# A state space stage re-ordered: its recurrence for two groups in complex pairs, its inputs turned inside SBUF, and modulations in four columns

## The chip, the cores and the metric

The kernel runs on one core of one Trainium2 chip. The metric is the device time of one execution in microseconds (us). The engines are TensorE (PE, matrix products), VectorE (DVE), ScalarE (ACT), GpSimd (POOL) and SyncE (SP, which only issues transfers here).

## The reference, cut to what matters

Two blocks work on 256 tokens of 1024 features, beside a context of 256 tokens. The change lies in the first block. Its first layer is an attention with 16 heads (MLA), its second is a state space layer (S5) with 128 groups of 64 complex states; one direction runs forward, one backward, and each runs through the context first and then through the tokens:

```python
for i in range(2):
    sh, sc, gt = split(silu(c) @ w_mod[i] + b_mod[i], 3)      # modulation, 1024 -> 3072
    h = x * (1 + sc) + sh                                     # also for the context, with c_ctx
    y = mla(h) if i == 0 else s5(h)
    x = layernorm(ALPHA * x + gt * y)

def s5(h):
    u, g = split(h @ w_in, 2)            # 1024 -> 2048 inputs u, 2048 gates g
    for direction in (forward, backward):
        x_t = lam_bar * x_{t-1} + b_bar @ u_t       # 128 groups x 64 complex states
        y  += real(c @ x_t)
    return ((ya * sigmoid(yb)) * silu(g)) @ w_out   # ya, yb = split(gelu(y) @ w_glu + b_glu, 2)
```

## The kernel before

**Products.** Activations and weights are split into a high and a low half in a reduced float32 format, and each product is three matmuls (`products`, lines 119 to 121: high by high, low by high, high by low). `weight` (line 88) fetches 512 KB of a weight with SyncE, ACT casts the high half (`wh`, line 97), DVE subtracts it (`wl`, line 98). The third matmul of each three needs `wl`.

**Modulation.** `mod` (line 577) multiplies silu(c) (32 columns, two of them used) by the weights `w_mod` in pieces of 256 KB. A piece is one matmul of 512 columns (part 0) or two of 256 (part 1), written to 32 rows of PSUM each. There are 64 pieces: 16 of part 1 for the first layer, worked off in the stage `mla_in`, and 48 for the second layer (32 of part 0, 16 of part 1) worked off between the heads. The start of the kernel does the first layer's part 0 with four matmuls of 128 columns in four column groups (`shift_scale`, line 678).

**The S5 stage.** Time is cut into blocks of 8 tokens: 32 blocks of context and 32 of tokens. The 128 groups are worked off in four parts b = 0..3 with four quarters a = 0..3 each:

- `u(b, j)` (line 1072): 48 matmuls make a 512 x 512 corner of the inputs, ACT copies it to SBUF (`s5_ut`, line 438) and stores it to DRAM (`d_u`, line 439); a transfer of GpSimd's queue loads it back in another layout (`s5_U`, line 446).
- `s5_blocks` (line 454): with operators loaded from DRAM (`s5_op<-d_rt`) 128 matmuls per quarter pair make the block sums, and ACT copies each bank to `s5_V` (line 475). The operators share one ring of five buffers with those of the outputs.
- `s5_scan` (line 480): the recurrence over the 63 blocks, on DVE. Real and imaginary parts lie apart, 32 columns of 63 blocks. A tree of 5 levels runs over the context, then seven single steps, then four steps of eight blocks with a table of powers (`s5_tab`, made by `s5_steps`, line 316). It takes 80 instructions a part (lines 493 to 497), and two copies (line 517).
- `s5_out` (line 520): `within` (line 536) adds what a block's own tokens give, `across` (line 549, operators `d_o`) what the states give, `close` turns the result back.

The emission order of PE and DVE is kept as written. `s5_layer` (line 1078) interleaves each scan with the next part's `u`, with `s5_blocks`, with the output of the part before, and with single gates (`gate`, line 955: 24 matmuls, stored to DRAM as `d_sg`). A scan runs right after its blocks, so that `across(b-1)` stands beside scan b. ACT and the queues follow a scheduler. After the last scan stand `across` of part 3 and the first product of the GLU.

## Time and profile before

| what | us |
|---|---|
| median of 3 runs | 1473.43 (1468.22 to 1474.59) |
| the profiled execution | 1472.76 |
| its span on the core | 1471.0 |
| start | 0 to 60 |
| `mla_in` | 60 to 216 |
| heads, with the second layer's modulation | 216 to 520 |
| layer norm, S5 inputs of part 0 | 520 to 612 |
| S5 stage | 612 to 858 |
| GLU | 858 to 1050 |
| second block | 1050 to 1471 |

The stages are read from the times at which their lines first run. Over the span PE is busy 92%, DVE 78%, ACT 48%, POOL 7%, and PE's mean granted clock is 0.958 of full speed. A busy share over a stage says how far an engine is from being its limit; which wait ended last there is read from the chain of waits and from the timeline.

### The profile page before, as it was taken

Reading aid. Unit: us, or ns where it says so; the run is one execution under the profiler, and the core shown is the slowest. Engines: PE = TensorE matmul, PEld = TensorE weight load, DVE = VectorE, ACT = ScalarE, POOL = GpSimd, SP = SyncE. Lnnn points to the kernel's source line nnn. Section 1 sums busy time; section 2 is a strip of 40 time slices with the busy share of each in tenths; the row PEclk is TensorE's granted clock in tenths of the full one; section 3 lists DMA queues with packets and bytes.
Section 4 is the critical chain, followed back from the end, with each engine's and each line's share of the span. In section 5 each row is a group of like instructions: output and inputs, shape, how many; then the busy total and the mean of one; then the engine's idle time right before and its main releaser. Section 6 shows DMA issues by size and latency. Waiting matters only on the chain.

```text
span 1471.0 us, 30448 instructions
## 1 busy us (share of the span) xinstructions
PE 1355.9 (92%) x12192; PEld 1199.6 (82%) x12192; DVE 1151.6 (78%) x2123; ACT 712.1 (48%) x1308; POOL 102.5 (7%) x225
## 2 busy tenths in 40 slices
PE   5979979999999998898787789999999999999997
PEld 4657657777788787898676689999999999999996
DVE  7989887888778889589988955655568876788887
ACT  4424336665455535432233354544347556655554
POOL 0012221111011101111111000000000000000000
PEclk8989998999999999999898889999999999999999
DMA  9469995555544543798778666566545453455552
GB/s 353 155 190 278 295 272 161 155 165 154 156 143 143 176 144 100 214 324 267 265 251 326 216 240 195 195 197 197 185 160 182 158 177 125 160 187 187 188 188 97
DMA packets 140623, 291.36 MB, mean 198 GB/s; under 512 B 30480, under 2 KB 70080, under 8 KB 135104
## 3 DMA queue, kind: packets, MB, share of 16 engines
q1 hardware_dynamic: 108592, 232.01, 47.5%
q0 software_dynamic: 11360, 49.34, 10.7%
q10 hardware_dynamic: 20528, 8.06, 2.0%
q8 instruction: 96, 1.57, 0.5%
q14 instruction: 47, 0.39, 0.1%
HBM read 234.83 MB, written 54.53 MB: 197 GB/s over the span
## 4 chain that ended last, share of the span: by engine, by line
PE 68%; DVE 14%; DMA 7%; issue 7%; ACT 3%; POOL 0%; SPq 0%; DVEq 0%; ACTq 0%; POOLq 0%
PE lin L121 14%; PE lin L120 14%; PE lin L119 14%; PE modps L591 3%; DVE s_t L493 2%; DVE wl L98 2%; DMA sp_x<-in_s_bcw_dram 2%; PE dn L121 1%; PE dn L119 1%; PE dn L120 1%; PE vps L472 1%; DMA d_o<-sp_o 1%; DVE s_V L495 1%; PE ptl L869 1%; PE slat L119 1%
## 5 line engine op out<-in xcount | busy, mean ns | idle before, releaser
L97 ACT CAST wh<-wr 128x1024 fp32r<-128x1024 f32 x268 | 280.7, 1049 | 412.1 <-PE lin L120 270.6
L98 DVE TENSOR_TENSOR wl<-wr,wh 128x1024 fp32r<-128x1024 f32 x268 | 327.7, 1224 | 150.4 <-ACT wh L97 149.8
L119 PE MATMUL lin<-prH,wh 128*128 128x256 f32 x512 | 145.9, 285 | 0.0
L119 PE MATMUL lin<-yaH,wh 128*128 128x256 f32 x512 | 145.5, 284 | 0.0
L121 PE MATMUL lin<-prH,wl 128*128 128x256 f32 x512 | 144.3, 282 | 1.0 <-DVE wl L98 1.0
L120 PE MATMUL lin<-yaL,wh 128*128 128x256 f32 x512 | 145.2, 284 | 0.0
L121 PE MATMUL lin<-yaH,wl 128*128 128x256 f32 x512 | 144.7, 283 | 0.0
L120 PE MATMUL lin<-prL,wh 128*128 128x256 f32 x512 | 144.3, 282 | 0.3 <-DVE prL L109 0.2
L120 PEld LDWEIGHTS lin<-prL,wh 128*128 128x128 f32 x512 | 97.3, 190 | 1.7 <-DVE prL L109 0.7
L119 PEld LDWEIGHTS lin<-prH,wh 128*128 128x128 f32 x512 | 97.4, 190 | 1.0
L119 PEld LDWEIGHTS lin<-yaH,wh 128*128 128x128 f32 x512 | 98.1, 192 | 0.0
L121 PEld LDWEIGHTS lin<-yaH,wl 128*128 128x128 f32 x512 | 98.1, 192 | 0.0
L120 PEld LDWEIGHTS lin<-yaL,wh 128*128 128x128 f32 x512 | 98.0, 191 | 0.0
L121 PEld LDWEIGHTS lin<-prH,wl 128*128 128x128 f32 x512 | 97.0, 189 | 1.2 <-DVE wl L98 1.2
L493 DVE TENSOR_TENSOR s_t<-s_V,s_tab 128x256 f32<-128x256 f32 (+2 forms) x120 | 73.0, 651 | 15.2 <-ACT s_V L475 13.9
L121 PE MATMUL u<-h,wl 128*128 128x256 f32 x224 | 65.1, 290 | 8.0 <-DVE wl L98 7.9
L121 PE MATMUL lin<-h,wl 128*128 128x256 f32 x128 | 43.3, 338 | 30.2 <-DVE wl L98 30.2
L427 POOL DMA_DIRECT2D d_t<-sp_g x128 | 66.8, 530 | 56.6 <-DVE sp_g L37 52.7
L120 PE MATMUL u<-h,wh 128*128 128x256 f32 x224 | 64.8, 289 | 1.6 <-issue 1.6
L119 PE MATMUL u<-h,wh 128*128 128x256 f32 x224 | 65.4, 292 | 0.0
L119 PE MATMUL lin<-hH,wh 128*128 128x512 f32 x144 | 61.7, 429 | 0.7 <-ACT hH L103 0.7
L37 DVE TENSOR_TENSOR sp_t<-s_pb,sp_x 128x1024 f32<-128x1024 f32 x64 | 60.2, 955 | 0.6
(505 smaller groups left out, 3862.2 us busy)
## 6 DMA issues: line engine op xcount, KB each, us to landing
wr<-in_glu_dram SPq DMA_DIRECT2D x64, 512.0 KB, 4.3
wr<-in_w_up_dram SPq DMA_DIRECT2D x44, 512.0 KB, 3.2
wr<-in_w_in_dram SPq DMA_DIRECT2D x32, 512.0 KB, 4.6
mraw<-in_w_mod_dram SPq DMA_DIRECT2D x64, 256.0 KB, 3.1
d_rt<-sp_rt SPq DMA_DIRECT2D x64, 256.0 KB, 4.1
d_o<-sp_o SPq DMA_DIRECT2D x32, 512.0 KB, 4.3
wr<-in_s_in_dram SPq DMA_DIRECT2D x32, 512.0 KB, 4.6
s_op<-d_o POOLq DMA_DIRECT2D x16, 1024.0 KB, 7.5
```

The lines of the kernel that those rows point to most:

```text
L37: return lambda *a, **k: self.net.in_order(f(*a, **k))
L97: self.in_order(nc.scalar.copy(hi, raw))
L98: self.in_order(nc.vector.tensor_tensor(lo, raw, hi.bitcast(F32), SUB))
L119: self.in_order(t.matmul(out, a[0], b[0], start=start, stop=False))
L120: self.in_order(t.matmul(out, a[0], b[1], start=False, stop=False))
L121: self.in_order(t.matmul(out, a[1], b[0], start=False, stop=stop))
L427: nc.gpsimd.dma_start(self.d_t[k].rearrange("s i j e c -> i s j e c")[:, :, j, e], a)
L472: self.in_order(nc.tensor.matmul(p[64 * e:64 * e + 64, c:c + 64], rt[:, d, j, r, 64 * e:64 * e + 64], u, start=True, stop=True, skip_group ...
L493: go(v.tensor_tensor(t[:, x], src.to_broadcast([128, 2, 32, n]), a[x].unsqueeze(1).to_broadcast([128, 2, 32, n]), MUL))
L495: go(v.tensor_tensor(dst, dst, t[:, 0], ADD))
L591: self.in_order(nc.tensor.matmul(p[32 * j:32 * j + 32, :w], self.cs[:, kc, :], raw[:, jj * w:jj * w + w], start=(kc == 0), stop=(kc == 7), ...
L869: self.in_order(nc.tensor.transpose(t[:, c], P[:, c], self.ident))
```

## The change

**Modulation.** The host lays `w_mod` out so that each piece of 256 KB is four blocks of 128 columns. `mod` issues four matmuls of 128 columns per piece, one to each group of 32 rows. The pieces, their bytes and their number are the same.

**The recurrence.** Real and imaginary part lie side by side (pairs of 8 bytes). A step is four DVE instructions: product with the real factor, sum, product of the swapped pair with the imaginary factor (with its signs), sum. `s5_context` runs the tree over the context of one part (five levels, 20 instructions on 1024, 512, 256, 128 and 64 elements); `s5_latents` runs 31 single steps for two parts together, 124 instructions on 128 elements each. All parts make 4 x 20 + 2 x 124 = 328 instructions; before there were 4 x 82.

**Inputs.** For parts 1 to 3 the store to `d_u` and the load of `s5_U` are replaced by eight SBUF to SBUF transfers per `u` on ACT's queue, 16 partitions each. Part 0 still goes through DRAM. `s5_ut` has one buffer there, where it had two.

**Order.** ACT copies each bank in two pieces (context sums to `s5_C`, the others to `s5_V`). The operators' ring has four buffers. All `u` and `s5_blocks` come first; `across` of parts 0 and 1 comes after the latents of the first pair, `across` of parts 2 and 3 after those of the second. Two clocks, estimates of PE's and of DVE's time, decide between which of them the DVE steps are emitted. Weights are fetched one or two products ahead, every second one of the first twelve into extra slots (`wx`). The 11 gates stand in the second half. The powers take 20 DVE and 16 ACT instructions, where there were 24 and 2.

```diff
-        hi, lo = (pool.tile([128, 1024], F32R, tag=tag + x, name=tag + x, bufs=bufs) for x in "hl")
+        if place is None:
...
+        hi, lo = place
         nc.sync.dma_start(raw, src)
...
+        for n, r, i in ((4, tr[:, :, 0], ti[:, :, 0]), (2, None, self.li)):
...
+                if r is not None:
+                    nc.scalar.copy(r[:, g].rearrange("p (d q) -> p d q", d=2), re)
+                for x in range(2):
+                    nc.scalar.mul(i[:, g, :, x].rearrange("p (d q) -> p d q", d=2), im, 2.0 * x - 1.0)
...
+        for k in range(4):
+            re, im = tr[:, :, k], ti[:, :, k, :, 1]
+            v.tensor_tensor(t[0], re, re, MUL)
+            v.tensor_tensor(t[1], im, im, MUL)
+            v.tensor_tensor(tr[:, :, k + 1], t[0], t[1], SUB)
+            for x in range(2):
+                v.scalar_tensor_tensor(ti[:, :, k + 1, :, x], re, 4.0 * x - 2.0, im, MUL, MUL)
...
-        nc.scalar.dma_start(self.d_u[b, j].rearrange("s p k -> p s k")[:, ::-1], ut.rearrange("p s g k -> p s (g k)"))
...
+    def s5_move_u(self, j, ps, U, tp):
+
+        ut = self.s5_turn_u(ps, tp, 1)
+        for s in range(8):
+            self.nc.scalar.dma_start(U[16 * s:16 * s + 16, j].rearrange("i q g k -> i (q g k)"),
+                                     ut[:, s].rearrange("p g k -> p (g k)"))
...
-        t = self.ops.tile([128, 2048], F32, name="s5_op", bufs=5)
+        t = self.ops.tile([128, 2048], F32, name="s5_op", bufs=4)
...
-                nc.scalar.copy(V[:, :, d, 4 * a:4 * a + 4, :].rearrange("p r q k -> p r (q k)"),
-                               p.rearrange("p (r c) -> p r c", r=2))
...
+            nc.scalar.copy(c[:, :, :, ::-1] if d else c, pv[:, :, :, 0:32])
+            nc.scalar.copy(x[:, :, :, 1 - d:32 - d], pv[:, :, :, 32 + d:63 + d])
+
+    def s5_step(self, a, src, swapped, t, base, dst):
+
+        v = self.nc.vector
+        for x, y, z in ((src, a[0], base), (swapped, a[1], dst)):
+            self.in_order(v.tensor_tensor(t, x, y.to_broadcast(t.shape), MUL))
+            self.in_order(v.tensor_tensor(dst, z, t, ADD))
...
+        for k in range(31):
+            c, o = (k, 31 - k), self.s5_column(V, (k + 1, 30 - k))
+            self.s5_step(a, self.s5_column(V, c), self.s5_column(V, c, swap=True), t, o, o)
+            yield 1.18
...
-                for q in range(4 * w // piece):
-                    raw = tp.tile([128, piece], F32, name="mraw", bufs=bufs)
-                    nc.sync.dma_start(raw, src[kc, :, q * piece:q * piece + piece])
...
+                for q in range(n):
+                    raw = tp.tile([128, 4, 128], F32, name="mraw", bufs=2)
+                    nc.sync.dma_start(raw, src[kc, q])
+                    for j in range(4):
                         self.in_order(nc.tensor.matmul(
-                            p[32 * j:32 * j + 32, :w], self.cs[:, kc, :], raw[:, jj * w:jj * w + w],
-                            start=(kc == 0), stop=(kc == 7), skip_group_check=True))
+                            p[32 * j:32 * j + 32, q * 128:q * 128 + 128], self.cs[:, kc, :], raw[:, j],
+                            start=(kc == 0 and q == 0), stop=(kc == 7 and q == n - 1), skip_group_check=True))
...
-            us = [self.u(1, j, h1) for j in range(2)]
             ahead = [self.operator(self.d_rt[a], nc.sync) for a in range(4)]
-            for j in range(2):
-                self.s5_store_u(1, j, us[j], tp)
-                self.s5_load_u(1, j, tp)
             self.s5_steps(tp)
             self.ordered = (mybir.EngineType.PE, mybir.EngineType.DVE)
-            st, prev = self.s5_blocks(0, tp, ahead), None
             for a in range(4):
-                st[2](a)
...
+                linear()
+                blocks(0, a)
+            linear()
+            within, across, close = out(0)
...
+            first = jobs[-1]
+            for a in range(4):
+                linear()
+                blocks(2, a)
+            linear()
+            for a in range(4):
+                blocks(3, a)
+                if a in (1, 2):
+                    linear()
+            last = jobs[-1]
+            scanned(first)
```

**DVE at the start of the S5 stage.** Before, from the last constants of the preparation (`sp_g`) on; the two `wl` are the low halves for `u(1, 0)` and `u(1, 1)`, and then comes the table of powers (`s_t` is its scratch tile, `s_tab` the table):

```order
L37 SCALAR_TENSOR_TENSOR sp_g<-dmask,dskip,sp_g 128x16 [waits Activation_49]
L98 TENSOR_TENSOR wl<-wr,wh 128x1024 [waits DMAHW6_49,PE_49,Activation_49]
L98 TENSOR_TENSOR wl<-wr,wh 128x1024 [waits DMAHW7_49,PE_49,Activation_49]
L332 TENSOR_TENSOR s_t<-s_tab 128x128 [waits DMASW7_49,DMAHW0_49,DMASW6_49,DMAHW2_49,DMASW5_49,DMAHW3_49,DMASW4_49,DMAHW4_49,DMASW3_49,DMAHW5_49,DMASW2_49,DMAHW6_49,DMASW1_49,DMAHW7_49,DMASW0_49,Activation_49]
L333 TENSOR_TENSOR s_t<-s_tab 128x128 [waits Activation_49]
L334 TENSOR_TENSOR s_tab<-s_t 128x128 [waits DVE_49]
```

After, the end of the powers (`s_tr` and `s_ti` are the new table) and the weights behind it; the first `wl` is that of `u(1, 0)`:

```order
L337 TENSOR_TENSOR s_t<-s_ti 128x128 [waits DVE_49]
L340 SCALAR_TENSOR_TENSOR s_ti<-s_tr,s_ti 128x4x32
L338 TENSOR_TENSOR s_tr<-s_t 128x4x32 [waits DVE_49]
L340 SCALAR_TENSOR_TENSOR s_ti<-s_tr,s_ti 128x4x32
L100 TENSOR_TENSOR wl<-wr,wh 128x1024 [waits PE_49]
L100 TENSOR_TENSOR wx<-wr,wx 128x1024
L100 TENSOR_TENSOR wl<-wr,wh 128x1024 [waits PE_49]
L100 TENSOR_TENSOR wx<-wr,wx 128x1024 [waits DMAHW1_49,Activation_49]
```

The `wl` of `u(1, 0)` stood ahead of the table; now it stands behind all 20 instructions of it, and the first of these still waits for the transfers of the stage ahead.

**ACT among the inputs.** Before, two inputs (`s_ut`, the copy in two pieces, and its store `d_u`) and the casts of weights between them:

```order
L438 COPY s_ut<-u 128x8x32 [waits DMAHW5_49,PE_49]
L438 COPY s_ut<-u 128x8x32
L439 DMA d_u<-s_ut 128x8x64 [waits DMAHW7_49,Activation_49]
L97 CAST wh<-wr 128x1024 [waits DMAHW5_49,DVE_49,PE_49]
L438 COPY s_ut<-u 128x8x32 [waits DMAHW2_49,PE_49]
L438 COPY s_ut<-u 128x8x32
L439 DMA d_u<-s_ut 128x8x64 [waits DMAHW1_49,Activation_49]
L97 CAST wh<-wr 128x1024 [waits DMAHW6_49,DVE_49,PE_49]
```

After, one input with its eight moves (`s_U<-s_ut`), and behind it a cast into an extra slot (`wx`) and the copies of block sums (`s_C`, `s_V`):

```order
L440 COPY s_ut<-u 128x8x32 [waits DMAHW4_49,DMAHW3_49,DMAHW5_49,DMAHW2_49,DMAHW6_49,DMAHW1_49,DMAHW7_49,DMAHW0_49,PE_49]
L440 COPY s_ut<-u 128x8x32
L99 CAST wh<-wr 128x1024
L458 DMA s_U<-s_ut 16x8x64 [waits Activation_49]
L458 DMA s_U<-s_ut 16x8x64 x5
L458 DMA s_U<-s_ut 16x8x64 [waits DMAHW2_49]
L458 DMA s_U<-s_ut 16x8x64 [waits DMAHW3_49]
L99 CAST wx<-wr 128x1024
L483 COPY s_C<-vps 128x2x128 [waits PE_49]
L484 COPY s_V<-vps 128x2x4x31
L483 COPY s_C<-vps 128x2x4x32 [waits PE_49]
```

The copy of an input now waits for the moves of the input ahead (`s_ut` has one buffer), the last of the eight moves waits for the first one's semaphore, and a cast and the copies of block sums stand behind them on ACT.

**PE between two parts.** Before, the blocks of part 2 (`vps`, from the inputs `s_U` and the operators `s_op`) stand behind a gate (`lin`):

```order
L119 MATMUL lin<-h_6368,wh 128x256
L120 MATMUL lin<-h_6368,wh 128x256
L121 MATMUL lin<-h_6368,wl 128x256
L472 MATMUL vps<-s_U,s_op 64x64 [waits DMASW5_49,DMASW4_49,PE_49]
L472 MATMUL vps<-s_U,s_op 64x64 x3
L472 MATMUL vps<-s_U,s_op 64x64 [waits DMASW6_49]
L472 MATMUL vps<-s_U,s_op 64x64
```

After, they stand right behind the last input of the part, `u(2, 3)`:

```order
L121 MATMUL u<-h_6827,wx 128x256
L122 MATMUL u<-h_6827,wx 128x256
L123 MATMUL u<-h_6827,wx 128x256
L477 MATMUL vps<-s_U,s_op 64x64 [waits DMAHW2_49,DMAHW3_49,DMAHW1_49,DMAHW5_49,DMAHW0_49,DMAHW6_49,DMASW1_49,DMAHW7_49,PE_49,Activation_49]
L477 MATMUL vps<-s_U,s_op 64x64
L477 MATMUL vps<-s_U,s_op 64x64 [waits DMAHW5_49,DMAHW4_49,DMAHW6_49,DMAHW3_49,DMAHW7_49,DMAHW1_49,DMAHW0_49]
L477 MATMUL vps<-s_U,s_op 64x64
```

The blocks' wait for their inputs moved from loads of an input made some products earlier to the moves of the product just ahead; part 3's blocks stand behind `u(3, 3)` in the same way, and part 1's last input has two outputs (`within`) behind it first.

## Rows read from the trace of the kernel before

**Rows 1.** Busy time by stage: the stretch in us from the span's start, its length, then for each engine the busy time and (x) its instructions, at the end PE's granted clock, the DMA engines' busy share and GB/s.

```profile
60.00:216.00 156.00, 136.62 (x1075) 98.94 (x1073) 135.44 (x204) 54.10 (x106) 33.00 (x76) 0.94 0.83 249
216.00:520.00 304.00, 301.06 (x2097) 229.88 (x2098) 249.45 (x461) 180.89 (x397) 30.67 (x69) 0.98 0.52 157
...
612.00:858.00 246.00, 196.16 (x3261) 182.15 (x3261) 199.97 (x383) 76.83 (x142) 28.40 (x51) 0.89 0.77 267
```

**Rows 2.** The chain of waits within 216 to 520 us (the heads), shares of these 304 us by engine and line.

```profile
by line: PE modps L591 12.7%; PE lin L119 6.2%; PE lin L120 6.0%; PE lin L121 6.0%; PE ptl L869 5.3%; PE slat L119 5.3%; PE slat L121 5.2%; PE slat L120 5.2%; PE rtps L400 4.4%; PE pv L119 4.2%; PE pv L120 3.5%; PE pv L121 3.5%; PE qabs L11
```

**Rows 3.** Timeline of PE (start in us, us, engine, line, operation, output<-inputs, shape, count; a float32 matmul is two records): four pieces of the start's modulation, then a piece of part 0 and a piece of part 1 in the heads, each with the matmul behind it.

```profile
33.91 1.08 PE L678 MATMUL modps<-mraw,cs 128*32 128x128 f32 x32
...
334.56 1.04 PE L591 MATMUL modps<-mraw,cs 128*32 128x512 f32 x2
335.53 1.09 PE L869 MATMUL ptl<-ident,P 128*128 128x128 f32 x8
...
492.40 0.63 PE L591 MATMUL modps<-mraw,cs 128*32 128x256 f32 x4
492.95 0.39 PE L119 MATMUL pv<-ptlH,ctH 128*128 128x256 f32 x1
```

**Rows 4.** The chain of waits within 60 to 216 us (`mla_in`), shares of these 156 us.

```profile
by line: DMA sp_x<-in_s_bcw_dram 14.5%; DMA d_o<-sp_o 11.5%; issue 9.5%; DVE sp_t L37 7.0%; DMA d_rt<-sp_rt 6.9%; DVE sp_o L37 6.2%; DVE sp_r L37 5.2%; PE lin L119 4.9%; PE lin L120 4.6%; PE lin L121 4.6%; DMA d_sg<-sg 4.2%; DVE wl L98 3.8%
```

**Rows 5.** Busy time in the four stretches from a scan's first instruction to its last (columns as in rows 1).

```profile
644.19:690.29 46.10, 41.27 (x513) 40.25 (x512) 45.24 (x88) 13.40 (x24) 8.40 (x15) 0.96 0.85 279
693.63:737.26 43.63, 32.94 (x517) 30.05 (x517) 42.70 (x86) 10.20 (x21) 5.16 (x10) 0.86 0.76 272
744.95:788.28 43.33, 31.64 (x592) 28.62 (x593) 42.40 (x86) 14.48 (x29) 5.16 (x10) 0.88 0.76 275
793.43:843.78 50.35, 36.08 (x513) 32.32 (x515) 48.03 (x91) 11.97 (x19) 3.76 (x7) 0.83 0.71 258
```

**Rows 6.** Groups of instructions by line and shape within the S5 stage (busy us, mean ns of one, idle time before them): `wl`, the gates' third matmuls, and the scan's products of 128 elements that lie a block column apart.

```profile
L121 PE MATMUL lin<-h,wl 128*128 128x256 f32 x88 | 31.1, 354 | 27.2 <-DVE wl L98 27.2
L98 DVE TENSOR_TENSOR wl<-wr,wh 128x1024 fp32r<-128x1024 f32 x25 | 30.5, 1218 | 14.8 <-ACT wh L97 14.8
...
L493 DVE TENSOR_TENSOR s_t<-s_V,s_tab 128x128 f32<-128x128 f32 x8 | 2.7, 381 | 0.1
```

**Rows 7.** Timeline of DVE: a chain of five dependent instructions on 128 elements; rows of the table of powers (single elements 32 bytes apart, then runs of two), each second of a pair reading what the first wrote; the `wl` and the scan behind it; what follows the last scan.

```profile
21.40 1.60 DVE L37 SCALAR_TENSOR_TENSOR lm_er<-lm_er,lm_sz 128x128 f32<-128x128 f32 x5
...
630.50 0.43 DVE L332 TENSOR_TENSOR s_t<-s_tab 128x128 f32<-128x128 f32 x1 [5.62 <-ACT s_tab L322]
...
631.29 0.41 DVE L334 TENSOR_TENSOR s_tab<-s_t 128x128 f32<-128x128 f32 x1
631.74 0.42 DVE L335 TENSOR_TENSOR s_t<-s_tab 128x128 f32<-128x128 f32 x1
...
633.32 0.42 DVE L333 TENSOR_TENSOR s_t<-s_tab 128x256 f32<-128x256 f32 x1
633.78 0.43 DVE L334 TENSOR_TENSOR s_tab<-s_t 128x256 f32<-128x256 f32 x1
...
641.87 1.21 DVE L98 TENSOR_TENSOR wl<-wr,wh 128x1024 fp32r<-128x1024 f32 x1
644.19 1.29 DVE L493 TENSOR_TENSOR s_t<-s_V,s_tab 128x512 f32<-128x512 f32 x2 [1.11 <-ACT s_V L475]
...
843.69 3.91 DVE L1132 TENSOR_TENSOR yaL<-y,yaH 128x512 fp32r<-128x512 f32 x6
```

**Rows 8.** Timeline of ACT and its queue (ACTq) at the start of the S5 stage.

```profile
616.82 1.05 ACT L97 CAST wh<-wr 128x1024 fp32r<-128x1024 f32 x1 [4.99 <-PE u L120]
...
622.58 1.05 ACT L97 CAST wh<-wr 128x1024 fp32r<-128x1024 f32 x1 [4.17 <-PE u L120]
...
624.20 0.37 ACTq L439 DMA_DIRECT2D d_u<-s_ut  x1
630.04 0.69 ACT L322 COPY s_tab<-s_lam 128x128 f32<-128x128 f32 x2 [5.88 <-DMA d_u<-s_ut]
...
634.10 1.05 ACT L97 CAST wh<-wr 128x1024 fp32r<-128x1024 f32 x1 [1.97 <-PE u L120]
...
643.57 0.59 ACT L475 COPY s_V<-vps 128x512 f32<-128x512 f32 x1 [0.35 <-PE vps L472]
```

**Rows 9.** Timeline of PE behind the last scan: `across` of part 3, the transposes, the first product of the GLU.

```profile
854.09 1.96 PE L549 MATMUL yps<-s_op,s_V 64*32 64x128 f32 x64 [0.66 <-DMA s_op<-d_o]
857.26 1.97 PE L560 MATMUL ytps<-ident,s_ysb 128*128 128x128 f32 x8 [1.21 <-ACT s_ysb L556]
858.88 0.56 PE L119 MATMUL lin<-yaH,wh 128*128 128x256 f32 x1
```

**Rows 10.** Transfers issued within the S5 stage: output<-input, queue, count, KB each, median us from issue to landing.

```profile
s_op<-d_o POOLq DMA_DIRECT2D x16, 1024.0 KB, 7.5
...
d_u<-s_ut ACTq DMA_DIRECT2D x15, 256.0 KB, 5.4
s_U<-d_u POOLq DMA_DIRECT2D x12, 256.0 KB, 4.5
...
d_sg<-s_sg ACTq DMA_DIRECT2D x11, 128.0 KB, 4.2
```

More of the change, by code (lines that the diff above doesn't have):

```diff
@@ L326, in s5_steps @@
[L326 to L337 removed]
+        self.tr = tr = tp.tile([128, 4, 5, 32], F32, name="s5_tr")
@@ L575, in cond, with mod @@
         self.lnb = self.load(self.gp, self.I["ln_b"], [128, 2, 8], "lnb", nc.gpsimd)
-    def mod(self, i, parts, m, tp, piece=512, bufs=2):
+    def mod(self, i, parts, m, tp):
         nc = self.nc
@@ L1096, in emit @@
                         nc.scalar.activation(yb[:, t0 + t], pv[:, t], AF.Gelu_apprx_tanh)
-                return self.s5_out(b, uvs, tp, emit)
-            def run(scan, us):
-                while scan and scan[1] < us:
-                    x = next(scan[0])
-                    if x is True:
-                        scan.clear()
-                    else:
-                        scan[1] += x
-                if scan:
-                    scan[1] -= us
+                return self.s5_out(b, U[b], V[b // 2], tp, emit, "ps" if b == 3 else "bg")
@@ L1110, in s5_layer, with high, low @@
+            def high(b):
+                for j in range(4 * b, 4 * b + 4, 2):
+                    nc.scalar.copy(ya[0][:, j:j + 2], y[0][:, j:j + 2])
+            def low(b):
+                for j in range(4 * b, 4 * b + 4, 2):
+                    self.in_order(nc.vector.tensor_tensor(ya[1][:, j:j + 2], y[0][:, j:j + 2],
+                                                          ya[0][:, j:j + 2].bitcast(F32), SUB))
+            U[0] = tp.tile([128, 4, 8, 2, 32], F32, name="s5_U", bufs=3)
             for j in range(4):
-                self.s5_load_u(0, j, tp, nc.sync)
@@ new lines, in s5_layer @@
+                linear()
[3 more added lines that the diff above has]
+            for a in range(4):
+                within(a)
+                if a == 1:
+                    linear()
+            blocks(1, 0)
+            linear()
+            for a in range(1, 4):
+                blocks(1, a)
+            first = jobs[-1]
+            for a in range(4):
+                linear()
+                blocks(2, a)
+            linear()
+            for a in range(4):
+                blocks(3, a)
+                if a in (1, 2):
+                    linear()
@@ new lines, in s5_layer @@
+            last = jobs[-1]
+            scanned(first)
+            clock[0] = max(clock)
+            y.append(self.big.tile([128, 16, 256], F32, tag="s16", name="y", bufs=3))
+            ya.append(self.big.tile([128, 16, 256], F32R, tag="s16", name="yaH", bufs=3))
+            for b in range(2):
+                for a in range(4):
+                    if b == 1:
+                        within(a)
+                    across(a)
+                    beside(2.2)
+                    if a % 2 == 1:
+                        linear()
+                close()
+                high(b)
+                beside(1.0)
+                within, across, close = out(b + 1)
@@ L1172, in s5_layer @@
+            final = out(3)
+            for a in range(4):
+                within(a)
+                final[0](a)
+                beside(1.2)
+                linear()
+            while asked[0] < len(linears) or parts:
+                linear()
+            scanned(last)
             ya.append(self.big.tile([128, 16, 256], F32R, tag="s16", name="yaL", bufs=3))
@@ L1174, in s5_layer @@
                 across(a)
-                if a < 3:
+                if a < 2:
                     low(a)
             close()
+            high(2)
+            for a in range(4):
+                final[1](a)
+            low(2)
+            final[2]()
             high(3)
             low(3)
-            assert self.gate_steps.gi_frame is None or next(self.gate_steps, True)
             self.ordered = (mybir.EngineType.PE,)
```

285 lines of the change are left out of this document (133 added, 152 removed).

## The prediction

> **What bounds the kernel now.** I read the busy times by stage first, then in each stage that the change touches the chain of waits or the timeline. In the heads (216 to 520 us) PE is busy 301.06 of 304.00 us and DVE 249.45 [rows 1], and the largest single entry of the chain there is the modulation, 12.7% or 38.6 us [rows 2]: what PE saves there shortens the stage, as long as DVE keeps up. In `mla_in` (60 to 216) PE has 19 us of slack and the chain runs through transfers and DVE's preparation of operators [rows 1, 4]. In the S5 stage (612 to 858) PE is busy 196 of 246 us [rows 1], but within the four scans DVE is busy 178 of 183.4 us [rows 5]: from 644.19 to 843.7 [rows 7] DVE sets the pace. The four stretches hold 88, 86, 86 and 91 instructions, 82 of each the scan's and the other 23 mostly `wl`. At some 1.2 us each [rows 6] these take 28 of the 183.4 us, and the scans alone 156 us.
>
> **Modulation.** Before, a piece of part 0 holds PE from 334.56 to 335.53, 0.97 us, and a piece of part 1 from 492.40 to 492.95, 0.55 us; four pieces of the start's form together take 1.08 us, 0.27 each [rows 3]. In the heads lie 32 pieces of the one kind and 16 of the other: 32 x 0.97 + 16 x 0.55 = 39.8 us, close to the chain's 38.6. After, 48 x 0.27 = 13.0. That is 26.8 us less for PE. DVE's 249 us would then stand in 277 instead of 304, 90% instead of 82%, and somewhere a short wait for it will come through; I take 25. The bounds are 12 (DVE's work becomes the last at half of the pieces) and 29 (a piece costs 0.22, its share of the row's 1.08 without the last matmul's own end). In `mla_in` 16 x 0.28 = 4.5 us of PE lie under the chain of transfers: I take 0, between 0 and 3. The pieces' transfers keep size and count. They are asked for sooner, at a DMA share of 0.52 [rows 1], which costs nothing.
>
> **The recurrence by itself.** A step after is four dependent instructions on 128 elements. The chain of five such instructions takes 1.60 us for the five with the last one's end, of which 0.29 is the end: (1.60 - 0.29) / 4 = 0.33 us from one to the next [rows 7]. 62 steps x 4 x 0.33 = 81 us. Of the tree's levels, the first is near `wl`'s 1.2 us an instruction, the one of 256 elements 0.46 (from 633.32 to 633.78, runs of two elements), the one of 128 elements 0.33, and those of 512 and 64 interpolate to 0.7 and 0.3: 4 x 3.0 = 12 us a part, 48 for all [rows 6, 7]. So DVE has 129 us of recurrence instead of 156: 27 us less, if pairs cost what contiguous elements cost. The nearest row on pairs is that of runs of two, 0.46 for 256 elements, which lies on the line between 128 and 512; the row against it is that of single elements, 0.45 for 128 [rows 7].
>
> The Trainium skill, "SBUF — State Buffer", section on door 1, says that SBUF is read in lines of 16 bytes and that full speed needs at least two hits a line. Each float32 pair gives just two, so by it the 81 us stand, and single elements 32 bytes apart are slow, as the rows show; were a pair still charged for its new line, it would be the second rival below.
>
> **Its start.** This is what the order changes most. Before, PE makes `u(1, 0)` and `u(1, 1)` from 622.58 to 634.10, 5.76 us each, then the blocks of part 0 until about 643.6, 9.5 us [rows 8], and the first scan starts at 644.19 [rows 7]. After, `wl` of `u(1, 0)` stands on DVE behind the table. The table waits for the last store of part 0's inputs: issued at 624.20, and ACT ran on at 630.04 [rows 8]. Then come 12 small copies on ACT (some 0.25 us each by the row of two in 0.69, so 3), 20 small DVE instructions (0.3 us each, 6) and `wl` (1.2): 640. PE's third matmul waits for it, so some 17 us of PE are lost. Then PE makes four `u` and the blocks of part 0, 4 x 5.76 + 9.5 = 32.5 us: the first tree starts at 672, 28 us later than the first scan. The gain of 27 us is spent there.
>
> **Its middle.** From 672 PE makes three `u`, four `within` (2 us together, from their share of records) and the blocks of part 1, 29 us: with the last tree, the first latents start at about 715. From there DVE has 81 us of latents, 24 us of two trees and 17 `wl` at 1.2, 126 us together: it could end at 841. PE reaches the blocks of part 3 near 771 (five `u`, 19 us of blocks, two gates of 24 matmuls, half of an input's 48, 2.9 us each, and the waits below), before DVE needs them, so PE's waits alone are covered. They come at the blocks of parts 2 and 3, right behind `u(2, 3)` and `u(3, 3)`: copy 0.7, eight issues of 0.37 on ACT's queue [rows 8] and a landing. No row shows a move inside SBUF; the nearest are 4.2 to 5.4 us for 128 and 256 KB to and from DRAM [rows 10]. With 4 us that is 8 us at each place. What is not covered: casts on ACT stand behind these moves, `wl` waits for the casts, and DVE keeps program order, so latents wait behind `wl`. Before, DVE lost 14.8 us that way in the whole stage [rows 6]. I take 8 us (0 if no cast is held up long, 20 if the landings take 5.4 us): the latents end at 849.
>
> The Trainium skill, "DMA: Bandwidth & Descriptors", section "Anatomy of one DMA", gives about 2 us for a transfer that small, most of it the receipt of the write, and heaviest in HBM. That would be an estimate of some 2.1 us here, and with it the term of 8 us would be 0; no transfer of this trace was that short in this stage.
>
> **Its end.** Before, from the last scan to the first product of the GLU, 843.69 to 858.88, lie 15.2 us [rows 7, 9]. After, two parts have to be closed. Four operators fit in the ring, so those of part 3 start to load when the first `across` of part 2 is through: 2 us (the 1.96 of a row [rows 9]), 7.5 for the landing [rows 10], 3 x 2.6 us for the next at the landing's pace, 2 for the last `across`, and some 3 for the transposes and the split, 857.26 to 858.88 and around it [rows 9]. That is 22 us; I take 21. GLU starts at 870 instead of 858.9: the stage is 12 us longer. Copies on ACT in two pieces, `s5_ut` with one buffer and four operators instead of five are covered by PE's 50 us of slack there, beyond what is counted; all gates move, none is added.
>
> **The sum.** 1472.8 (the profiled execution, 0.7 below the median) - 25 + 0 + 12 = 1459.8, so 1460. PE's clock is granted at 0.89 of full speed in the S5 stage and 0.98 in the heads [rows 1]: longer waits there would not speed it up, and I put no term on it.
>
> **Rivals.**
>
> - *The start's wait is covered.* If PE's lost 17 us are not on the path (the latents start at 700 and ACT's small copies are quick), the stage gets 15 to 20 us shorter than forecast. For it: the table's copies are small. Against it: the wait for the landing at 630.04 stands in the trace, and the order puts `wl` behind it. 1460 - 20 = 1440.
> - *Slower: a pair costs a strided access.* Place: the 248 instructions of the latents. At 0.45 us, the row of single elements, they take 112 us instead of 81, +30 us, all on DVE's path: 1490. For it: each pair lies 256 bytes from the next, further than any run of two in the trace. Against: the row of runs of two. It makes the kernel slower by more than 0.5% (7.4 us, about what a measurement can tell from no change) from 0.33 + 21 / 248 = 0.41 us on.
> - *The moves land late.* At 5.4 us, as the stores to DRAM, copy, issues and landing take 9 us, longer than an input and its quarter of blocks (5.76 + 2.4), and with one buffer each input waits for the one ahead: 12 x 1 us and longer waits at both blocks, DVE behind them. +12 to 15 us: 1474.
> - *The modulation doesn't do what it says for the time.* DVE and ACT in the heads become last; half of the gain is left: 1472. Against it: PE stands there 3 us of 304 [rows 1].
>
> **How the numbers follow.** Forecast 0.48, covered start 0.16, late moves 0.14, strided pairs 0.13, modulation 0.09. The forecast's own range is 1448 to 1472. The whole one takes in the covered start and most of the strided pairs: 1438 to 1488. Faster by over 0.5% (below 1466) is most of the forecast (0.38), the covered start and a little of the others: 0.57. Within 0.5% (1466 to 1481) is the rest of the forecast, the late moves and the halved modulation: 0.28. Slower: 0.15.
>
> **What would show it.** In the profile after: modulation pieces of 0.27 us and heads of about 279 us; a wait of PE for `wl` of some 17 us after the inputs of part 0; the first tree near 647 (672 less the heads' 25); instructions of 128 elements 0.33 us apart in the latents; waits of PE at the blocks of parts 2 and 3; 20 us from the last latent step to the GLU. The prediction is wrong if DVE's waits in the heads eat the modulation's gain, if pairs cost 0.41 us or more, or if the first tree starts before 660 by the old times.

## The result, and the profile after

The changed kernel takes 1492.92 us in the median of four runs (1488.39 to 1498.13), the kernel before 1472.90; the ratio is 1.0142 with a 95% interval of 1.0102 to 1.0183. It is slower by 20 us, and the forecast was 1460, faster, with a range to 1488.

The profiled execution has a span of 1491.3 us beside 1471.0. Three marks in both traces split the 20.3 us: the last product of the operators' preparation with its inputs (`sp_t<-s_pw`), at 605.7 before and 586.9 after; the first product of the GLU, 858.88 [rows 9] and 881.24; the end. Up to the first mark 18.8 us are gained, the S5 stage between the two takes 294.3 us instead of 253.2, 41.1 more, and 2.0 us are gained behind it. The forecast had -25, +12 and 0. The first mark of the thirteen profiles with the new modulation lies between 580.0 and 589.4, so one profile gives the gain ahead of it to some 5 us.

**The heads.** Busy times by stage (columns as in [rows 1]), of the heads and of the S5 stage after:

```profile
216.00:501.00 285.00, 279.03 (x2349) 229.83 (x2349) 247.91 (x461) 180.13 (x398) 30.77 (x69) 0.98 0.57 169
593.00:881.20 288.20, 199.39 (x3280) 187.05 (x3279) 153.79 (x379) 80.32 (x191) 22.14 (x39) 0.83 0.63 218
```

Timeline of PE after, two modulation pieces in the heads with the matmul behind each:

```profile
335.75 0.43 PE L600 MATMUL modps<-mraw,cs 128*32 128x128 f32 x8
336.11 0.51 PE L121 MATMUL qrope<-qnH,wh 128*128 128x512 f32 x1
...
493.29 0.43 PE L600 MATMUL modps<-mraw,cs 128*32 128x128 f32 x8
493.64 0.39 PE L121 MATMUL pv<-ptlH,ctH 128*128 128x256 f32 x1
```

A piece holds PE 0.36 us, where [rows 3] had 0.97 and 0.55: 48 x 0.36 = 17.3 us instead of 39.8, a gain of 22.5. DVE has the same 248 us in a shorter stage, 87% instead of 82%, and PE waits 6.0 us of 285 where it waited 2.9 of 304 [rows 1].

**The S5 stage.** DVE has 46 us less to do than before (153.79 beside 199.97 [rows 1]), and the stage is longer. Timeline of DVE after:

```profile
664.54 1.23 DVE L100 TENSOR_TENSOR wl<-wr,wh 128x1024 fp32r<-128x1024 f32 x1 [10.61 <-ACT wh L99]
665.68 1.22 DVE L490 TENSOR_TENSOR s_t<-s_C,s_tr 128x1024 f32<-128x1024 f32 x1
...
698.87 1.23 DVE L100 TENSOR_TENSOR wx<-wr,wx 128x1024 fp32r<-128x1024 f32 x1 [18.56 <-ACT wx L99]
...
713.15 0.29 DVE L490 TENSOR_TENSOR s_t<-s_V,s_lam 128x128 f32<-128x128 f32 x1
713.48 0.30 DVE L491 TENSOR_TENSOR s_V<-s_V,s_t 128x128 f32<-128x128 f32 x1
...
772.07 1.23 DVE L100 TENSOR_TENSOR wl<-wr,wh 128x1024 fp32r<-128x1024 f32 x1 [23.20 <-ACT wh L99]
...
860.01 2.49 DVE L1173 TENSOR_TENSOR yaL<-y,yaH 128x512 fp32r<-128x512 f32 x4
```

Read against [rows 7]: an instruction of the latents stands 0.33 us behind the last one, as forecast. But the first tree starts 78.8 us after the first mark (665.7 - 586.9), where the first scan started 38.5 us after it: 40 us lost. From there to the last step DVE needs 194.4 us instead of 199.6, a gain of only 5. It stands 18.56 us and 23.20 us for a low half whose cast has not come. Timeline of ACT and its queue after, from the first input of part 1 on, and around the last two inputs:

```profile
623.92 0.65 ACT L440 COPY s_ut<-u 128x256 f32<-128x256 f32 x2 [11.90 <-PE u L123]
624.59 5.21 ACTq L458 DMA_DIRECT2D s_U<-s_ut  x8
629.85 0.40 ACT L483 COPY s_C<-vps 128x256 f32<-128x256 f32 x1 [5.29 <-issue]
...
634.13 0.65 ACT L440 COPY s_ut<-u 128x256 f32<-128x256 f32 x2 [2.12 <-PE vps L477]
634.66 0.41 ACT L483 COPY s_C<-vps 128x256 f32<-128x256 f32 x1
634.81 6.58 ACTq L458 DMA_DIRECT2D s_U<-s_ut  x8
641.43 0.39 ACT L484 COPY s_V<-vps 128x248 f32<-128x248 f32 x1 [6.36 <-DMA s_U<-s_ut]
...
643.75 0.65 ACT L440 COPY s_ut<-u 128x256 f32<-128x256 f32 x2 [0.43 <-DMA s_U<-s_ut]
...
656.45 6.13 ACTq L458 DMA_DIRECT2D s_U<-s_ut  x8
662.62 0.40 ACT L484 COPY s_V<-vps 128x248 f32<-128x248 f32 x1 [5.90 <-issue]
...
663.44 1.07 ACT L99 CAST wh<-wr 128x1024 fp32r<-128x1024 f32 x1
...
665.09 10.84 ACTq L458 DMA_DIRECT2D s_U<-s_ut  x8
675.97 0.40 ACT L483 COPY s_C<-vps 128x256 f32<-128x256 f32 x1 [9.97 <-issue]
...
742.91 0.65 ACT L440 COPY s_ut<-u 128x256 f32<-128x256 f32 x2 [0.26 <-DMA s_U<-s_ut]
748.35 5.13 ACTq L458 DMA_DIRECT2D s_U<-s_ut  x8
...
770.99 1.05 ACT L99 CAST wh<-wr 128x1024 fp32r<-128x1024 f32 x1 [2.27 <-PE lin L122]
```

Eight moves hold ACT 5.1 to 10.8 us, where the store they replace held it 0.37 [rows 8]. Copies of block sums (three times of the first four with `s_C` done and `s_V` not) and the next cast stand behind them. The eight issues alone cost 5: the view of line 458 gives durations in ns (min/median/max) for all 96.

```profile
L458 ACTq DMA_DIRECT2D s_U<-s_ut x96: 554/620/1317, 624.6 to 760.2; - x96
```

What this does to the start is seen from PE's timeline below: its last block of part 0 ends at 649.77 (647.69 + 2.09), and the first tree starts 15.9 us later. The last copies of block sums, the cast and the low half ahead of the tree come behind the moves of 656.45. Before, the first scan stood 0.7 us behind PE's last block.

PE's waits are the other side of it. Timeline of PE after: the low half of `u(1, 0)`, the last block of part 0, the blocks of part 2, those of part 3, and the stage's end:

```profile
616.59 0.58 PE L123 MATMUL u<-h,wl 128*128 128x256 f32 x1 [10.97 <-DVE wl L100]
...
647.69 2.09 PE L477 MATMUL vps<-s_U,s_op 128*64 128x64 f32 x64
...
706.89 3.04 PE L477 MATMUL vps<-s_U,s_op 128*64 128x64 f32 x52 [7.34 <-DMA s_U<-s_ut]
...
742.94 0.48 PE L477 MATMUL vps<-s_U,s_op 128*64 128x64 f32 x4 [1.89 <-DMA s_U<-s_ut]
...
755.08 0.48 PE L477 MATMUL vps<-s_U,s_op 128*64 128x64 f32 x4 [11.65 <-DMA s_U<-s_ut]
...
762.40 3.89 PE L477 MATMUL vps<-s_U,s_op 128*64 128x64 f32 x68 [6.84 <-DMA s_U<-s_ut]
...
881.24 0.56 PE L121 MATMUL lin<-yaH,wh 128*128 128x256 f32 x1
```

At the blocks of part 3 PE waits three times, 20.4 us: not one input is late but three, each behind the one ahead. DVE's second wait hangs on this: its cast (770.99) stood for PE's next product, not for ACT's moves. From the last step to the GLU lie 21.2 us (860.01 to 881.24), as forecast. PE's granted clock over the stage is 0.83, where it was 0.89 [rows 1].

The chain of waits after, within 740 to 770 us, shows what a late input is made of:

```profile
743.85 1.22 DVE wl L100
745.09 3.18 DMA wr<-in_s_in_dram
...
752.20 0.63 ACTq L458
752.86 1.98 DMA s_U<-s_ut
755.01 0.66 ACT s_ut L440 x2
756.28 0.62 ACTq L458
...
760.18 1.98 DMA s_U<-s_ut
762.40 5.60 PE vps L477 x116
```

Copy 0.66, issues of 0.62 to 0.66 apart, and 1.98 us for the last one's landing, then the next copy: 7.4 us an input in series (755.01 to 762.40), against PE's 5.76. The input ahead of it lost 4.8 us more: its copy was done at 743.56, and its first move waited until 748.35 for a weight's transfer (issued at 745.09) that had used the same semaphore.

A landing of 1.98 us is that of a quiet stretch: from 740 to 765 us the DMA engines are busy 0.19. The view of the transfers in the stage and the chain of waits within 590 to 882 us (its shares by line, and three of its pieces):

```profile
s_U<-s_ut ACTq DMA_DIRECT2D x96, 32.0 KB, 3.8
```

```profile
by line: issue 21.5%; DMA s_U<-s_ut 11.2%; DVE s_t L490 9.3%; ACTq L458 8.2%; DVE s_V L491 5.7%; DMA wr<-in_s_in_dram 4.1%; PE u L123 3.4%; PE vps L477 3.3%; DMA s_op<-d_t 3.3%; PE u L121 3.3%; DMA s_op<-d_o 3.2%; PE u L122 3.2%; DVE s_C L4
...
644.42 5.75 DMA s_U<-s_ut
...
665.79 8.91 DMA wr<-in_s_in_dram
675.32 7.45 DMA s_U<-s_ut
```

The median landing is 3.8 us, and in the first half of the stage (DMA share 0.57 from 625 to 645, 0.68 from 645 to 666) some take twice that. On this chain the landings of moves have some 33 of the 292 us, their issues 24, and weights' transfers 12; one of these, issued at 665.79, held up the last two moves of an input until 674.72. So the issues are one part of what an input costs; landings behind one buffer are the other.

### The profile page after: what moved, and what is told of

Its sections match the earlier page's. It is cut to its first block, busy times and chain, and to the rows that moved or that the text cites. A ratio compares the mean times of both kernels' runs of the same rounds, so it can differ in the third digit from the quotient of the medians.

```text
span 1491.3 us, 31286 instructions
## 1 busy us (share of the span) xinstructions
PE 1329.0 (89%) x12512; PEld 1199.4 (80%) x12512; DVE 1103.7 (74%) x2119; ACT 715.6 (48%) x1354; POOL 96.3 (6%) x213
## 4 chain that ended last, share of the span: by engine, by line
PE 65%; DVE 14%; DMA 9%; issue 6%; ACT 3%; ACTq 2%; POOL 0%; SPq 0%; DVEq 0%; POOLq 0%
PE lin L121 14%; PE lin L122 14%; PE lin L123 14%; DMA s_U<-s_ut 2%; DVE wl L100 2%; DVE s_t L490 2%; DMA sp_x<-in_s_bcw_dram 2%; ACTq L458 2%; DVE sp_t L37 1%; DMA mraw<-in_w_mod_dram 1%; PE dn L123 1%; DMA d_o<-sp_o 1%; PE dn L121 1%; PE dn L122 1%; DVE s_V L491 1%
## 5 line engine op out<-in xcount | busy, mean ns | idle before, releaser
L100 DVE TENSOR_TENSOR wl<-wr,wh 128x1024 fp32r<-128x1024 f32 x262 | 320.3, 1223 | 179.4 <-ACT wh L99 178.8
L99 ACT CAST wh<-wr 128x1024 fp32r<-128x1024 f32 x262 | 274.4, 1049 | 345.1 <-PE lin L122 241.3
L477 PE MATMUL vps<-s_U,s_op 128*64 128x64 f32 x1024 | 39.8, 242 | 39.1 <-DMA s_U<-s_ut 27.7
L477 PEld LDWEIGHTS vps<-s_U,s_op 128*64 128x64 f32 x1024 | 36.8, 155 | 42.1 <-issue 28.5
L37 DVE TENSOR_TENSOR sp_t<-s_pw,sp_x 128x1024 f32<-128x1024 f32 x64 | 59.7, 953 | 0.8
L122 PE MATMUL lin<-hL,wh 128*128 128x512 f32 x144 | 57.9, 402 | 0.5 <-DVE hL L106 0.5
L123 PE MATMUL lin<-hH,wl 128*128 128x512 f32 x144 | 57.7, 401 | 0.0
```

What stands on the lines that cost most here:

```text
L37: return lambda *a, **k: self.net.in_order(f(*a, **k))
L99: self.in_order(nc.scalar.copy(hi, raw))
L100: self.in_order(nc.vector.tensor_tensor(lo, raw, hi.bitcast(F32), SUB))
L122: self.in_order(t.matmul(out, a[0], b[1], start=False, stop=False))
L123: self.in_order(t.matmul(out, a[1], b[0], start=False, stop=stop))
L477: self.in_order(nc.tensor.matmul(p[64 * e:64 * e + 64, c:c + 64], rt[:, d, j, r, 64 * e:64 * e + 64], U[:, j, 2 * a + e].rearrange("p g k ...
```

## The experiments

The first theory was that the issues hold ACT. The rivals were that the data land late (with the single buffer), and that the order is at fault. The runs stand on several chips, on which the kernel before took 1468.1 to 1472.9; the ratios allow for that, and differences of medians between runs, as the text gives them, can be off by some 5 us. The last columns are of each profile: from the first mark to the first instruction of the recurrence, from there to the end of its last step, and from there to the GLU, in us.

| run | median us | ratio to before (95%) | first | recurrence | end | sum |
|---|---|---|---|---|---|---|
| before | 1472.90 | | 38.5 | 199.6 | 15.1 | 253.2 |
| after | 1492.92 | 1.0142 (1.0102 to 1.0183) | 78.8 | 194.4 | 21.1 | 294.3 |
| mod_only | 1451.63 | 0.9879 (0.9846 to 0.9912) | 43.6 | 195.9 | 13.9 | 253.4 |
| moves16 | 1548.66 | one run | 97.0 | 231.5 | 20.9 | 349.4 |
| moves_sp | 1490.27 | 1.0155 (1.0122 to 1.0188) | 63.4 | 210.0 | 20.9 | 294.3 |
| ut2 | 1481.52 | 1.0082 (1.0054 to 1.0109) | 73.5 | 185.3 | 21.8 | 280.6 |
| ut2_sp | 1466.93 | 0.9992 (0.9973 to 1.0010) | 83.2 | 165.4 | 21.6 | 270.2 |
| dram_u | 1469.43 | 0.9996 (0.9975 to 1.0017) | 62.7 | 186.3 | 21.2 | 270.2 |
| order_late | 1472.65 | 1.0020 (0.9996 to 1.0045) | 73.1 | 180.1 | 20.3 | 273.5 |
| dram_late | 1456.16 | 0.9916 (0.9888 to 0.9944) | 63.6 | 175.4 | 21.2 | 260.2 |
| wl_first | 1489.63 | 1.0147 (1.0110 to 1.0183) | 71.3 | 206.5 | 20.2 | 298.0 |
| dram_late_wl | 1454.67 | 0.9904 (0.9870 to 0.9938) | 61.5 | 173.6 | 21.4 | 256.5 |
| early_lat | 1457.07 | 0.9907 (0.9883 to 0.9932) | 64.0 | 172.8 | 22.4 | 259.2 |
| early_moves | 1482.13 | 1.0089 (1.0061 to 1.0117) | 70.7 | 190.5 | 21.7 | 282.9 |

**mod_only.** The kernel before with the new `mod` and its weights' layout, nothing else.

```diff
...
-                            p[32 * j:32 * j + 32, :w], self.cs[:, kc, :], raw[:, jj * w:jj * w + w],
...
+                            p[32 * j:32 * j + 32, q * 128:q * 128 + 128], self.cs[:, kc, :], raw[:, j],
...
```

> The kernel before with the modulation in four columns as its only change. If the loss lies in the S5 stage alone (theory and rivals agree on that), the heads and mla_in end 19 us earlier as in the changed kernel, the S5 stage takes its old 246 us, and the time is 1472.9 - 19 - 2 = 1452, between 1449 and 1456. If the earlier end of the heads is itself paid back later, by collisions of transfers for instance: 1465 to 1473.

It took 1451.63, 19 us less than the kernel before on the same chip (1470.86; 13 to 23 by the interval). The S5 stage has its old length, 253.4. The modulation's gain is real and stays; the loss is the S5 stage's.

**moves16.** Each move cut in two of 8 partitions, the same bytes.

```diff
-            self.nc.scalar.dma_start(U[16 * s:16 * s + 16, j].rearrange("i q g k -> i (q g k)"),
-                                     ut[:, s].rearrange("p g k -> p (g k)"))
+            for h in range(2):
+                self.nc.scalar.dma_start(U[16 * s + 8 * h:16 * s + 8 * h + 8, j].rearrange("i q g k -> i (q g k)"),
+                                         ut[64 * h:64 * h + 64, s].rearrange("p g k -> p (g k)"))
```

> The changed kernel with each move of an input cut into two of 8 partitions: 16 issues an input on ACT instead of 8, same bytes, same order. Theory (issues hold ACT): an input holds ACT some 5 us longer, if an issue costs 0.62 us whatever its size; with the first tree behind four and the waits at the blocks of parts 2 and 3, 30 to 50 us longer, 1520 to 1545. Rival landing (it is the data's way that counts): 1488 to 1500.

1548.66, a little beyond the theory's figure. The view of the moves' line and the timeline of ACT of this run:

```profile
L459 ACTq DMA_DIRECT2D s_U<-s_ut x192: 623/624/1351, 624.1 to 814.6; - x192
```

```profile
624.09 11.18 ACTq L459 DMA_DIRECT2D s_U<-s_ut  x16
```

Half the size costs the same 0.62 us: an issue is paid for by number, not by size. The first tree stands 28.4 us behind PE's last block of part 0, where it stood 15.9 in the change.

**moves_sp.** The moves on SP's queue.

```diff
-            self.nc.scalar.dma_start(U[16 * s:16 * s + 16, j].rearrange("i q g k -> i (q g k)"),
+            self.nc.sync.dma_start(U[16 * s:16 * s + 16, j].rearrange("i q g k -> i (q g k)"),
```

> The changed kernel with the 96 moves of inputs issued by SP in place of ACT. Theory (the issues hold ACT: eight take 5.1 to 10.8 us, and copies of block sums and casts stand behind them): ACT is free, the first half of the stage gets 20 to 30 us shorter, 1463 to 1473. Rival landing (the inputs' data come late, one buffer): the landings stay, 1488 to 1495. Rival order (the blocks stand too close behind their inputs, and DVE and PE wait for each other in program order whatever the queue): 1486 to 1495. Weights on SP's queue would then stand behind the moves, which could take back 5 to 10 us under each.

1490.27, the rivals' figure. The first tree does come 15 us earlier (0.5 us behind PE's last block of part 0), but all of it is lost again. Timelines of SP and of PE of this run:

```profile
692.69 5.04 SPq L458 DMA_DIRECT2D s_U<-s_ut  x8
697.83 0.54 SPq L98 DMA_DIRECT2D wr<-in_s_in_dram  x1
```

```profile
691.99 0.48 PE L477 MATMUL vps<-s_U,s_op 128*64 128x64 f32 x4 [4.38 <-DMA s_U<-s_ut]
699.45 0.48 PE L477 MATMUL vps<-s_U,s_op 128*64 128x64 f32 x4 [6.98 <-DMA s_U<-s_ut]
707.10 3.04 PE L477 MATMUL vps<-s_U,s_op 128*64 128x64 f32 x52 [7.17 <-DMA s_U<-s_ut]
```

The issues take 5.0 us there too, and each input still waits for the landing of the one ahead: 7.5 and 7.7 us from one wait's end to the next (691.99, 699.45, 707.10). A free ACT alone doesn't cure it, so the theory as put was too narrow, and the single buffer came under suspicion.

**ut2 and ut2_sp.** Two buffers for an input's copy, with the moves on ACT and on SP.

```diff
-        ut = self.s5_turn_u(ps, tp, 1)
+        self.s5_turn_u(ps, tp, 1, ut)
...
+            turned = tp.tile([128, 2, 8, 2, 32], F32, name="s5_ysb", bufs=1)
...
-                    self.s5_move_u(j, self.u(w, h1), U[b], tp)
+                    self.s5_move_u(j, self.u(w, h1), U[b], tp, turned[:, n % 2])
```

> The changed kernel with two buffers for an input's turned copy (they lie in the tile of the later outputs, so they are called s_ysb in the trace); 96 moves on ACT in the same order. What this tells apart: with one buffer each input goes copy 0.65, eight issues 5.0, last landing 2.0 us in series, 7.6 us against PE's 5.8. Theory now (a moved input costs its issues, 5 us of a queue that nothing overlaps, and ACT holds them): the copies no longer wait for the landing, 2 us an input, 3 to 10 us faster, 1480 to 1490. Rival (one buffer is what makes the inputs pile up): the waits of 20 us at the blocks of part 3 and 7 to 11 us at part 2 go, 15 to 30 us faster, 1463 to 1478.

> Two buffers as above, and the moves on SP. With SP alone the first tree came 20 us earlier and the end did not, since inputs of parts 2 and 3 queued up behind one buffer (7.5 us each) and weights behind moves. Theory (issues are the price: 5.0 us an input on whatever queue): copies run ahead of the queue, PE waits less at the blocks of parts 2 and 3, 1473 to 1485. Rival (one buffer): both waits gone, 1460 to 1472. If weights behind the moves are what counts on SP: 1485 to 1492.

On ACT the second buffer is worth 11 us (1481.52, the theory's side: the issues still hold ACT), on SP 23 (1466.93, the rival's side). PE's timeline in ut2_sp at the blocks of part 2, where moves_sp waited 18.5 us:

```profile
688.62 0.34 PE L478 MATMUL vps<-s_U,s_op 128*64 128x64 f32 x4 [2.95 <-DMA s_U<-s_ysb]
...
693.25 3.04 PE L478 MATMUL vps<-s_U,s_op 128*64 128x64 f32 x52 [4.29 <-DMA s_U<-s_ysb]
```

The issues and the single buffer act together: taking the issues off ACT alone brings 3 us and the second buffer alone 11, both 26. What the second buffer takes away is the wait of a copy for the landing ahead, so the landing is a part of the loss. In ut2_sp the first tree still comes late (83.2 us): a copy of an input on ACT waits 7.2 us for moves ahead to land there, and block sums and casts stand behind it.

**dram_u.** Inputs of parts 1 to 3 through DRAM as before, with the one buffer of the change for their copies.

```diff
-                    self.s5_move_u(j, self.u(w, h1), U[b], tp)
+                    self.s5_store_u(j, self.u(w, h1), tp, b)
+                    self.s5_load_u(j, U[b], b, nc.gpsimd)
```

> The changed kernel with the inputs of parts 1 to 3 through DRAM as before: one store a product on ACT, one load on GpSimd's queue. Theory (issues hold ACT): 11 fewer products with 5 us of issues on ACT, 1465 to 1478, though store and load together land some 9 us after the copy, so that the two waits of PE at the blocks of parts 2 and 3 stay. Rival landing: the way through DRAM lands later than the moves (3.8 us after the last issue), so slower, 1495 to 1510. Rival order: 1488 to 1500.

1469.43: 23 us faster than the change, though store and load are two transfers of 3.2 and 4.2 us each where a move lands in 3.8 (medians). One issue on ACT beats eight, and the first tree stands 0.7 us behind PE's last block of part 0. This speaks for the theory. Against the rival it says only that a longer way of the data by itself isn't what costs: the copy of an input waits here for the store alone, not for the load.

**order_late.** One product more ahead of the blocks of parts 2 and 3 (an input at part 2, a gate at part 3), moves as in the change.

```diff
+            linear()
             for a in range(4):
                 linear()
                 blocks(2, a)
-            linear()
             for a in range(4):
+                if a in (0, 1):
+                    linear()
                 blocks(3, a)
-                if a in (1, 2):
-                    linear()
```

> The changed kernel with one more input product ahead of the blocks of parts 2 and 3, so that the blocks don't stand right behind their own last input; moves on ACT as they are. Theory (issues hold ACT): only the two waits of 11.7 us of PE shrink by a product's 5.8 us each, 1478 to 1487. Rival order: these two waits and the two of DVE behind them (18.6 and 23.2 us) go, 1455 to 1470. Rival landing: 1478 to 1487.

1472.65, between the two: the order has a part of its own, some 20 us. **dram_late** has both this and the way through DRAM.

> Inputs of parts 1 to 3 through DRAM and one more input product ahead of the blocks of parts 2 and 3, together. Theory (two causes: ACT's issues, which delay the first tree by 19 us, and blocks right behind their own inputs, which stretch the first latents by 22 us): nearly additive, 1470 - 20 = 1448 to 1455. Rival (both remove the same wait): 1465 to 1470.

1456.16, just above the theory's range, and 37 us faster than the change where the two alone brought 23 and 20. In the S5 stage of the profiles it is 34 us, where they brought 24 and 21 (last column): the two share a part of what they remove.

**wl_first** and **dram_late_wl** fetch the first two weights ahead of the table.

```diff
+            self.ordered = (mybir.EngineType.PE, mybir.EngineType.DVE)
+            fetch(2)
             self.s5_steps(tp)
-            self.ordered = (mybir.EngineType.PE, mybir.EngineType.DVE)
```

> The changed kernel with the first two weights fetched and split ahead of the table of powers, so that DVE's low half for the first input product stands ahead of it as before; nothing else. Theory: PE's wait of 11 us for it goes; as ACT then holds the path, 4 to 11 us faster, 1482 to 1489. Rival (the start's wait is covered, the first tree waits for ACT's moves only): 1490 to 1494.

> The same with the first two weights ahead of the table as well. Theory: the first tree starts some 10 us earlier and nothing but PE stands ahead of it: 8 to 11 us faster than without, 1438 to 1447, faster than the kernel before with the modulation alone (1452). Rival (start covered): no difference to the run without.

1489.63 and 1454.67. PE's wait of 11 us for the low half goes, but PE then waits 6.8 and 1.8 us (6.7 and 1.6) for the loads of part 0's inputs. The first tree comes 7 us (on ACT's moves) and 2 us (through DRAM) earlier, and the totals move by 3 and 2 us, inside the intervals: the start's wait is nearly covered, and the expectation for the second run was wrong.

**early_lat** and **early_moves** start from the order of dram_late_wl and put two inputs behind the blocks of part 1 instead of ahead of them, through DRAM and with moves. Five inputs stay ahead of these blocks.

```diff
             for a in range(4):
                 within(a)
-                if a == 1:
-                    linear()
-            blocks(1, 0)
-            linear()
-            for a in range(1, 4):
+            for a in range(4):
                 blocks(1, a)
             first = jobs[-1]
             linear()
+            linear()
+            linear()
```

> The run with inputs through DRAM, late blocks and weights ahead of the table, and two input products fewer ahead of the blocks of part 1 (they follow behind these blocks). Theory (with ACT's queue free, PE's work ahead of the first latents is what spends the recurrence's 27 us): the latents start some 8 to 12 us earlier and the whole ends as much earlier, 1442 to 1448, faster than the kernel before with the modulation alone (1452). Rival (the blocks of part 1 then wait for their own inputs, or DVE for low halves): 1450 to 1458.

> The same order and the same early weights, but with the changed kernel's moves on ACT in place of the way through DRAM. Theory (issues of 5 us an input hold ACT): four inputs ahead of the first latents instead of seven, but each still holds ACT, and part 1's blocks wait for the last of them: 12 to 20 us slower than through DRAM, 1456 to 1468. Rival (only the order mattered): equal to the run through DRAM within 4 us.

1457.07, no gain, the rival's figure; and 1482.13 with moves, 25 us slower than through DRAM with the same order, and slower than either expectation had it. It is slower than order_late, too, by some 10 us. The order doesn't heal the moves.

## Why the prediction was wrong

The forecast missed by 33 us: 12 in the start of the S5 stage, 17 between the first tree and the last step, 6 in the modulation, and 2 the other way behind the stage.

**Modulation: mechanism right, size off.** Forecast 25 us (12 to 29), measured 19. The term took 0.27 us for a piece from four pieces in a row; one alone among other matmuls takes 0.36. That leaves 22.5, and PE's waits in the heads grew by 3.

**The recurrence by itself: right.** 0.33 us from one instruction to the next. The Trainium skill's page "SBUF — State Buffer", section on door 1, by whose rule two hits in a line of 16 bytes are enough for full speed, agrees with that.

**Its start: right for PE, wrong for ACT.** Forecast was that the recurrence begins 28 us later; it was 40. On PE the sum held: its last block of part 0 ends 62.9 us behind the first mark (37.8 before), 25 us later. The wait for the low half was shorter than forecast (11 us for 17, the table's instructions follow each other in 0.2 us). The rest is the 15.9 us by which the first tree stands behind that block, and for which the prediction had no term: the copies of block sums stood behind the moves on ACT. Inputs came 9.6 to 12.0 us apart there (their copies start at 623.92, 634.13, 643.75 and 655.78), where PE made one, with its quarter of blocks, in 8.0. Without moves on ACT (moves_sp, dram_u) the 15.9 us are 0.5 and 0.7. PE's clock, for which the prediction put no term, cost little here: the input right behind the wait of 11 us took PE 7.3 us, the next ones 6.0.

**Its middle: the step that failed, there as at the start.** The prediction gave an issue 0.37 us, the row of another transfer, counted the issues into the lateness of one input but not as time of ACT, and said that the copies on ACT and the single buffer "are covered by PE's 50 us of slack". An issue took 0.62, eight of them 5 us, and with 12 inputs ACT stood 60 us in issues alone, with the copies of block sums and the casts behind them. DVE lost 41.8 us in two waits for casts, where the term had 8: the first cast stood behind moves on ACT, the second behind PE's wait at part 3. The sum for one late input (8 us) was about right, at 7.4, but as three inputs stood in series behind one buffer, PE waited 20 us at part 3 and not 8. moves16 and dram_u show the issues, ut2 (and ut2_sp beside moves_sp) the buffer, order_late the blocks right behind their inputs. How the loss divides between issues and landings isn't shown: on the chain landings have the larger share, 33 us beside 24. The rival of late moves named this place and this mechanism, each input waiting for the one ahead, and put 14 us on it; that part of its reason holds, and it too had the issues at 0.37.

The landing was taken at 4 us, and the median was 3.8. The prediction's 2.1 us, worked out from the Trainium skill, "DMA: Bandwidth & Descriptors", section "Anatomy of one DMA", are near the 1.98 us of the last move in a quiet stretch and far from the 5.75 and 7.45 us on the chain; that section's figure is for transfers that GpSimd issues. Setting the term to 0 by it would have made the forecast worse. One transfer of that stage before was as short, against what the prediction says: a gate's store at 829.8 landed in 1.7 us.

**Its end: right**, 21 us.

**What the recurrence is worth.** With the moves gone and the order changed (dram_late, which keeps the one buffer) DVE's recurrence takes 175.4 us where mod_only takes 195.9, 20 us less; but it begins 20.0 us later and its end is 7.3 us longer. These are near the prediction's own terms for start and end (28 and 6), and no order tried here won them back. The fastest version by the median is mod_only. dram_late, dram_late_wl and early_lat beat the kernel before as well and lie 3 to 5 us above mod_only, with intervals that overlap its own, so no gain of the re-ordered stage over the old one is shown.

**Open.** What an issue's 0.62 us depends on was not settled beyond size and queue: fewer than eight moves an input weren't tried. Two buffers with inputs through DRAM weren't tried either, nor moves whose semaphores are not shared with weights' transfers. The ring of four operator buffers and the split copies were not changed by themselves.

## What to carry to other kernels

Count the issues of a transfer that is cut up, at the price of a row of the same form, on the queue of the engine that has to issue them, and name what stands behind them there: eight short moves held ACT five us where one long store held it 0.4. Here two transfers through DRAM were better than one way inside SBUF that an engine in the path had to issue piece by piece. One buffer makes each landing a part of the next input's time, so take the landing from a stretch as busy as the one it will be in. A faster recurrence gains nothing if what feeds it starts later by as much: add up when its first input is there, before its steps.

## What the runs showed of the hardware

- An issue of a move inside SBUF took 0.62 us on ACT's queue and 0.60 on SP's, the same for 32 KB on 16 partitions and 16 KB on 8, where a store of 256 KB from 128 partitions took 0.37.
- Such a move landed 3.8 us after its issue in the median of 96: 1.98 us for the last of an input from 740 to 765 us, where the DMA engines were busy 0.19, and 5.75 and 7.45 us on the chain in the first half of the stage, where they were busy 0.57 to 0.68.
